# Hybrid decoder step: output product begun on half the tokens, taps' input in 8 transfers, late slots in the scan

## Chip, cores, metric

One Trainium2 chip, one core. The metric is the device time of one execution in microseconds (us); the kernel before took 1579.87 us, median of three runs (1579.34 to 1582.29).

## The reference

One inference step of a two-layer trunk for 512 prompt tokens and 8 x 8 sample tokens, which share the weights; model width 1024. In short:

```python
# layer 0 (even mixer)
a_val, a_gate, q, k, v = split(rmsnorm(x) @ w_in)
u = a_val * sigmoid(a_gate)
c = silu(layernorm(causal_dwconv(concat(conv_hist, u), conv_w, conv_b), ln_g, ln_b))   # width 31, 512 channels
o = sliding-window attention (window 128, 8 query heads on 2 key heads, sinks, partial rotary)
x = x + concat(c, o) @ w_out
x = x + conv_ffn(rmsnorm(x))             # gate, width-3 depthwise conv, silu, times up, down
# layer 1 (odd mixer)
z, xbc, dt = split(rmsnorm(x) @ w_in)
xs, B, C = split(silu(causal_dwconv(concat(hist, xbc))))   # width 4
y, new_state = ssd_scan(xs, softplus(dt + bias), -exp(a_log), B, C, state)   # chunks of 128, 32 heads, 4 groups
y = grouped_rmsnorm((y + d_skip * xs) * silu(z))
x = x + y @ w_out
x = x + conv_ffn(rmsnorm(x))
```

Besides the two outputs the new histories and states are returned: last convolution rows, last 128 keys and values, scan states.

## The kernel before

**Layout.** Features lie on partitions, the 576 tokens (512 + 64) on the free axis, processed as two halves of 288 (`HALF`). Every dense product runs as three matmuls in a split float32 form, `mm3`: weights and activations are each cut into a high part (a copy on ScalarE, L150 for weights, L170 for activations) and a rest (a subtraction on VectorE, L151 and L171); then high x high (L160), high x rest (L161), rest x high (L162). Weights come in 512 KB loads (L141) into three rotating buffers. `units` computes input projections one 128-row output tile at a time; `out_proj` does an output product tile by tile and half by half and adds each result to the residual x on VectorE (`add_x`, L259). The order of instructions on each engine is made when the kernel is built, by a planner that knows the dependencies; SP (SyncE) issues all transfers in one queue, in order.

**Slots.** Most working tiles come from a pool of 48 equal slots in SBUF, 59 after the first mixer. `S` takes the slot that was freed longest ago and `free` puts one at the end of the list. A tile that takes a slot waits until the last reader of the slot's former tile is done, a store included.

**First mixer (`mix0`).** Input projections for gate and value of four channel tiles i = 0 to 3, keys, values, queries; between them attention in blocks of 128 queries: `scores` (with softmax on VectorE, ScalarE and GpSimd), then `values` (transposes L648, copies `ptb` L650, product `po` L653, results `of` L661). The width-31 convolution runs on VectorE for channel tiles 0 and 2 (`conv_taps`, L436, one instruction per tap) and on TensorE for 1 and 3 (`pe_conv`). `pe_conv` writes the padded channel tile to DRAM (`cad`) and loads it back four times, shifted by 0 to 3 tokens, for each of four groups of 32 channels: 32 transfers (L551, L552), each of 32 rows. Eight tap steps follow, each with four 32-column matmuls side by side (L559 for prompt, L566 for sample tokens). After the last block (`sample_scores`, `values(3)`, `sample_values`) `of` is split into pairs `oh`, the LayerNorm over 512 channels runs (mean by matmuls with a matrix of 1/512, L758, squares L762, `rstd` with L182 and L193, scale L765, swish L766, split into `cc`), then the output product for the attention rows (on `oh`), and at last that for the Conformer rows (on `cc`, pairs `ch` and `cl` in the profile).

**Second mixer (`mix1`).** Four groups of eight heads. `ssd(g)` is a generator with 28 steps: it builds chunk states `hst` and stores the final one (`ssm_p`, L1001), then per pair of heads loads decay rows (`acb`, L1018, and `ea2`, L1031, from DRAM), turns them into decays (ScalarE L1022 and L1023, VectorE L1024) and multiplies them into `yp` (L1048). Sample states `h0` are loaded (L1063), updated (L1090) and stored (`ssm_s`, L1091). `run(main, side)` lets the generator go step by step and emits side work between: in group 0 four gate units (z) and two B/C units, in groups 1 and 2 the eight output tiles of the group before and then four gate units, in group 3 gate units and four output tiles, evenly spread over 30 steps. The previous group's eight split tiles are freed with the eighth output tile. `gate` then gates, normalizes and splits.

Of the kernel before, what the change touches and what calls it, by code (L numbers as in the profile page):

```python
# [8 lines left out]
F32 = mybir.dt.float32  # L9
# [41 lines left out]
class Builder:  # L51
# [3 lines left out]
    def __init__(self, nc, tc, d, stack):  # L55
        self.nc, self.tc, self.d = nc, tc, d
        self.const = stack.enter_context(tc.tile_pool(name="const", bufs=1))
        self.xp = stack.enter_context(tc.tile_pool(name="xp", bufs=1))
        self.wp = stack.enter_context(tc.tile_pool(name="wp", bufs=1))
        self.sp = stack.enter_context(tc.tile_pool(name="sp", bufs=1))  # L60
        self.pp = stack.enter_context(tc.tile_pool(name="pp", bufs=1, space=bass.MemoryType.PSUM))
        self.dp = stack.enter_context(tc.tile_pool(name="dp", bufs=1, space=bass.MemoryType.DRAM))
        self.rings = {"mm": [0, 1, 2, 3], "aux": [4, 5, 6, 7]}
        self.idle = list(range(self.NSLOT))
        self.used = {}


    def S(self, name, n=T, dt=F32, rows=P):

        i = self.idle.pop(0)  # L70
# [5 lines left out]
    def free(self, *tiles):  # L76
        for t in tiles:
            if isinstance(t, (list, tuple)):
                self.free(*t)
            else:  # L80
                self.idle.append(self.used.pop(id(t))[0])

# [269 lines left out]
    def mix0(self):  # L352
# [22 lines left out]
        def a_gate(i):  # L375
            def go(half, p):
                if half == 0:
                    sg[i] = self.S("sg")
                    cap[i] = self.segp.tile([P, 542], F32, tag="capp", bufs=1, name="cap") if i in PC else self.S("cap", 542)
# [9 lines left out]
        segs = {}  # L389
        PC, NPTB = (1, 3), 3  # L390

        cad = {i: self.dp.tile([P, 846], F32, name=f"cad{i}") for i in PC}

# [9 lines left out]
        def a_val(i):  # L403
            def go(half, p):
# [3 lines left out]
                else:  # L408
# [5 lines left out]
                    if i in PC:  # L414
                        nc.sync.dma_start(cad[i][:, 0:542], cap[i])
                        nc.sync.dma_start(cad[i][:, 542:846].rearrange("p (b c) -> p b c", c=38), cas_v[i])
                    else:
# [119 lines left out]
        def pe_conv(i):  # L537
# [7 lines left out]
            xs4 = [xsp[c // 2][:, (c % 2) * 304:(c % 2) * 304 + 304] for c in range(4)]  # L545
            src = cad[i]
            for c in range(4):
                for j in range(4):
                    n = 540 if j < 3 else 536
                    r, rc = slice(j * 32, j * 32 + 32), slice(c * 32, c * 32 + 32)  # L550
                    nc.sync.dma_start(xp4[c][r, 0:n], src[rc, j:j + n])  # L551
                    nc.sync.dma_start(xs4[c][r, 0:304 - j], src[rc, 542 + j:846])  # L552
            yield
            pp, ps = self.pm(), self.pm()
            for s in range(8):
                k = slice(0, P if s < 7 else 96)
                for c in (3, 2, 1, 0):
                    w = w4[s // 4][k, (s % 4 * 4 + c) * 32:(s % 4 * 4 + c) * 32 + 32]
                    m = nc.tensor.matmul(pp[c * 32:c * 32 + 32, :], w, xp4[c][k, 4 * s:4 * s + NP], start=s == 0, stop=s == 7)  # L559
                    if s or c < 3:  # L560
                        self.tc.keep_in_program_order(m)
            for s in range(8):
                k = slice(0, P if s < 7 else 96)
                for c in range(4):
                    w = w4[s // 4][k, (s % 4 * 4 + c) * 32:(s % 4 * 4 + c) * 32 + 32]
                    m = nc.tensor.matmul(bt(ps[c * 32:c * 32 + 32, 0:64]), w, xs4[c].rearrange("p (b t) -> p b t", t=38)[k, :, 4 * s:4 * s + 8],  # L566
                                         start=s == 0, stop=s == 7)
# [164 lines left out]
        self.units([then_taps(val_unit(3), 2)], 1)  # L732
        self.norm_end()
        sample_scores()
# [8 lines left out]
        oh = [self.pair("o") for _ in range(4)]  # L743
        for j in range(4):
            self.split(of[j], oh[j])
        self.free(of)
# [3 lines left out]
        some_taps(99)  # L750
        lrs = self.S("lrs")
        csq = [self.S("csq") for _ in range(4)]
        cc = [self.pair("c") for _ in range(4)]
        for half in (0, 1):
            sl = HALF[half]
            pm = self.ps("pm")
            for i in range(4):
                nc.tensor.matmul(pm[:, :HB], self.o512, ca[i][:, sl], start=i == 0, stop=i == 3)  # L758
            for i in range(4):
                nc.vector.tensor_tensor(ca[i][:, sl], ca[i][:, sl], pm[:, :HB], op=SUB)  # L760
# [8 lines left out]
        self.free(oh, list(ca.values()), cas, lrs, csq)  # L769
        self.norm_begin("norm_f0", True)  # L770
# [4 lines left out]
    def mix1(self):  # L775
# [139 lines left out]
        def ssd(g):  # L915
# [85 lines left out]
            nc.sync.dma_start(d["ssm_p"][g], H[3])  # L1001
            self.free(H.pop(), btok)
            yield
# [79 lines left out]
            def finish(bh, behind):  # L1083

                for b4 in range(4):
# [71 lines left out]

        def run(main, side):
# [13 lines left out]
        for g in range(4):  # L1172
# [3 lines left out]
            if g:  # L1176
# [20 lines left out]
            run(ssd(g), side)  # L1197
            ys = gate(g, xs)
# [18 lines left out]
def build(nc, tc, d):  # L1217
    from contextlib import ExitStack
    with ExitStack() as stack:
# [15 lines left out]
def constants():  # L1235
# [12 lines left out]
    put("prot", prot)  # L1248
    put("m32", np.tile(np.eye(32, dtype=f), (4, 1)))
    half = np.arange(P) // 64  # L1250
# [131 lines left out]
```

## Time and profile before

| | |
|---|---|
| median of three runs | 1579.87 us |
| the profiled execution | 1580.21 us, span 1578.4 us, mean granted clock 0.997 |
| TensorE busy | 1547.4 us (98%) |
| VectorE busy | 997.7 us (63%) |
| ScalarE busy | 642.0 us (41%) |
| GpSimd busy | 146.9 us (9%) |
| HBM read, written | 140.54 MB, 15.21 MB |

The span is one profiled execution, from the first to the last instruction. Busy shares are means over stages with different limits; a stage is read by its own stretch of time. PE is TensorE's matmuls, PEld its weight loads, DVE VectorE, ACT ScalarE, POOL GpSimd, SP the queue of transfers. A row of stretches gives start:end, length, busy us (and instructions) of PE, PEld, DVE, ACT, POOL, then the granted TensorE clock as a share of full speed, the DMA share and GB/s. A row of the order of time gives start, duration, engine, line, what is written from what, and in brackets how long the engine had been idle and what ended that. A row of groups gives a count, busy us and mean ns. A float32 matmul shows as two records.

### The profile page before, as it was taken

What the parts mean: (1) busy time and instruction counts of PE and PEld (TensorE: products, weight loads), DVE (VectorE), ACT (ScalarE), POOL (GpSimd) and SP (SyncE); (2) the same over time, 40 slices, a digit from 0 to 9 for tenths busy, and PEclk for the clock granted to TensorE, in tenths of its full rate; (3) what the DMA queues carried; (4) which work ended last, traced back from release to release, by engine and by line L of the source; (5) the groups of instructions that cost most, each with busy time, mean ns of one, the idle gap of its engine ahead of it and who ended that gap; (6) DMA issues with size and microseconds to landing.
All of it is one profiled execution on the core that took longest, in us unless ns stands there. A gap on an engine that the chain in (4) does not pass through costs nothing. (4 is left out here: it accounts for less than half of the span.)

```text
span 1578.4 us, 28672 instructions
## 1 busy us (share of the span) xinstructions
PE 1547.4 (98%) x11709; PEld 1478.0 (94%) x11709; DVE 997.7 (63%) x1750; ACT 642.0 (41%) x1197; POOL 146.9 (9%) x362
## 2 busy tenths in 40 slices
PE   8999999999999999999998999999999999999999
PEld 7966799999999999998997998998999999999998
DVE  7968586553465355677796777776975653653552
ACT  6257373221222122476765555556542321221220
POOL 0026001000000000011202002002010000000000
PEclk9999999999999999999999999999999999999999
DMA  7514223222222222225345235235322222222222
GB/s 224 127 43 111 75 69 103 87 88 81 81 80 82 93 78 76 78 83 162 122 123 163 94 106 178 94 110 171 112 81 81 81 81 81 89 77 91 81 84 76
DMA packets 69841, 157.60 MB, mean 100 GB/s; under 512 B 20158, under 2 KB 24510, under 8 KB 69710
## 3 DMA queue, kind: packets, MB, share of 16 engines
q1 hardware_dynamic: 69710, 155.77, 32.2%
q8 instruction: 92, 1.51, 0.4%
q14 instruction: 39, 0.32, 0.1%
HBM read 140.54 MB, written 15.21 MB: 99 GB/s over the span
## 5 line engine op out<-in xcount | busy, mean ns | idle before, releaser
L160 PE MATMUL mm<-hh,wh 128*128 128x288 f32 (+1 forms) x2288 | 681.6, 298 | 9.0 <-ACT wh L150 7.7
L162 PE MATMUL mm<-hh,wl 128*128 128x288 f32 x2288 | 679.9, 297 | 0.0
L161 PE MATMUL mm<-hl,wh 128*128 128x288 f32 (+1 forms) x2288 | 678.6, 297 | 0.0
L160 PEld LDWEIGHTS mm<-hh,wh 128*128 128x128 f32 (+1 forms) x2288 | 430.2, 188 | 15.1 <-ACT wh L150 8.2
L150 ACT ACTIVATE wh<-wr 128x1024 fp32r<-128x1024 f32 (+1 forms) x215 | 223.4, 1039 | 537.8 <-issue 265.4
L161 PEld LDWEIGHTS mm<-hl,wh 128*128 128x128 f32 (+1 forms) x2288 | 430.9, 188 | 2.0 <-DVE hl L360 0.3
L162 PEld LDWEIGHTS mm<-hh,wl 128*128 128x128 f32 x2288 | 429.8, 188 | 2.9 <-issue 1.5
L151 DVE TENSOR_TENSOR wl<-wr,wh 128x1024 fp32r<-128x1024 f32 (+1 forms) x215 | 259.8, 1209 | 81.5 <-ACT wh L150 81.3
L161 PE MATMUL mm<-yl,wh 128*128 128x288 f32 x960 | 287.0, 299 | 0.2 <-DVE yl L171 0.2
L160 PE MATMUL mm<-yh,wh 128*128 128x288 f32 x960 | 286.3, 299 | 0.7 <-DVE x L259 0.7
L162 PE MATMUL mm<-yh,wl 128*128 128x288 f32 x960 | 284.5, 297 | 0.4 <-DVE wl L151 0.4
L160 PEld LDWEIGHTS mm<-yh,wh 128*128 128x128 f32 x960 | 181.6, 190 | 4.3 <-DVE x L259 1.8
L161 PEld LDWEIGHTS mm<-yl,wh 128*128 128x128 f32 x960 | 182.0, 190 | 2.8 <-issue 1.4
L162 PEld LDWEIGHTS mm<-yh,wl 128*128 128x128 f32 x960 | 181.6, 189 | 1.6 <-issue 0.9
L259 DVE TENSOR_TENSOR x<-x,mm 128x288 f32<-128x288 f32 x192 | 85.3, 451 | 153.1 <-PE mm L162 152.8
L304 DVE TENSOR_TENSOR gbuf<-mm,rs 128x224 f32<-128x224 f32 x44 | 17.2, 391 | 108.9 <-PE mm L162 108.9
L315 ACT ACTIVATE gsilu<-gconv,par 128x512 f32<-128x512 f32 x44 | 31.8, 724 | 115.8 <-DVE gconv L312 115.8
L312 DVE SCALAR_TENSOR_TENSOR gconv<-gbuf,par,gconv 128x592 f32<-128x592 f32 x88 | 73.1, 831 | 1.5
L325 DVE TENSOR_TENSOR gsilu<-mm,gsilu 128x288 f32<-128x288 f32 x88 | 40.0, 455 | 50.7 <-PE mm L162 50.7
L801 DVE SCALAR_TENSOR_TENSOR cconv<-cbuf,par,cconv 128x600 f32<-128x600 f32 x72 | 60.2, 840 | 11.6 <-ACT cconv L799 10.7
L1022 ACT ACTIVATE acb<-acb,ac 128x128 f32<-128x128 f32 x128 | 41.4, 390 | 50.6 <-DMA acb<-acd 34.4
L307 POOL COPY fpo<-gbuf 128x2 f32<-128x2 f32 x44 | 12.4, 281 | 476.0 <-DVE gbuf L304 476.0
(306 smaller groups left out, 1603.1 us busy)
## 6 DMA issues: line engine op xcount, KB each, us to landing
wr<-in_w_gate SPq DMA_DIRECT2D x44, 512.0 KB, 3.3
wr<-in_w_up SPq DMA_DIRECT2D x44, 512.0 KB, 3.3
wr<-in_w_in_o SPq DMA_DIRECT2D x40, 512.0 KB, 3.4
wr<-in_w_down SPq DMA_DIRECT2D x32, 448.0 KB, 3.4
wr<-in_w_down SPq DMA_DIRECT2D x16, 512.0 KB, 3.6
acb<-acd SPq DMA_DIRECT2D x32, 256.0 KB, 4.2
h<-in_h SPq DMA_DIRECT2D x32, 256.0 KB, 3.7
out_ssm_s<-h SPq DMA_DIRECT2D x32, 256.0 KB, 2.4
```

The lines of the kernel that those rows point to most:

```text
L150: nc.scalar.activation(hi[:, :n], raw[:, :n], AF.Copy)
L151: nc.vector.tensor_tensor(lo[:, :n], raw[:, :n], hi[:, :n].bitcast(F32), op=SUB)
L160: nc.tensor.matmul(out, hi[:, ws], xh[:, sl], start=i == 0, stop=False)
L161: nc.tensor.matmul(out, hi[:, ws], xl[:, sl], start=False, stop=False)
L162: nc.tensor.matmul(out, lo[:, ws], xh[:, sl], start=False, stop=i == n - 1)
L259: nc.vector.tensor_tensor(self.x[m][:, sl], self.x[m][:, sl], p[:, :HB], op=ADD)
L304: nc.vector.tensor_tensor(g[:, 290:514], p[:, 0:224], rs[:, HB:NP], op=MUL)
L312: nc.vector.scalar_tensor_tensor(cv[:, :592], g[:, k:592 + k], w(k), cv[:, :592], op0=MUL, op1=ADD)
L315: nc.scalar.activation(sl[:, :NP], cv[:, :NP], AF.Silu, bias=b)
L325: nc.vector.tensor_tensor(sl[:, HALF[half]], p[:, :HB], sl[:, HALF[half]], op=MUL)
L801: nc.vector.scalar_tensor_tensor(cv[:, :600], g[:, k:600 + k], w(k), cv[:, :600], op0=MUL, op1=ADD)
L1022: nc.scalar.activation(acb[:, cs], acb[:, cs], AF.Relu, bias=ac[:, o:o + 1], scale=-1.0)
```

## The change

In the first mixer:

- `oh` is made in two halves. The first half of the output product's tiles 0 to 5 is emitted between the last attention steps (`o_tile`, `o_split`), the second half and tiles 6 and 7 after the LayerNorm.
- The LayerNorm adds the four channel tiles on VectorE first (`lsum`, and the squares into `csq[0]`), so that one matmul each, in place of four, forms mean and square sums.
- `pe_conv` loads its input in 8 transfers: each reads 32 rows of `cad` at four shifts by one access pattern and writes 128 partitions, now ordered channel by shift. `cad` rows have 850 columns, with a zero after the prompt part and three zeros at the end, written by two small stores; the taps' weights and the constant `m32` are reordered to match, and the last tap step uses all 128 rows, with a zero weight for the 32nd tap.

In the slots: each free slot has a turn number, and `S` takes the lowest. `free(..., late=n)` puts a slot n turns further back; used for the final chunk state (8) and the sample states (6), both freed while their store is under way. The 11 extra slots enter with turn 0, ahead of the others.

In the second mixer `run` gets explicit places: over 28 steps, in groups 1 and 2 the output tiles in the first half (at k/16) and the gate units in the second (at 0.5 + k/8); in group 0 at k/6, in group 3 at (k+1)/9.

```diff
+        i = self.idle.pop(self.idle.index(min(self.idle, key=lambda e: e[0])))[1]
+        self.taken += 1
...
-                self.idle.append(self.used.pop(id(t))[0])
+                self.idle.append((self.taken + late, self.used.pop(id(t))[0]))
...
-        cad = {i: self.dp.tile([P, 846], F32, name=f"cad{i}") for i in PC}
+        cad = {i: self.dp.tile([P, 850], F32, name=f"cad{i}") for i in PC}
+        for i in PC:
+            nc.sync.dma_start(cad[i][:, 847:850], zeros)
...
             for c in range(4):
-                for j in range(4):
-                    n = 540 if j < 3 else 536
-                    r, rc = slice(j * 32, j * 32 + 32), slice(c * 32, c * 32 + 32)
-                    nc.sync.dma_start(xp4[c][r, 0:n], src[rc, j:j + n])
-                    nc.sync.dma_start(xs4[c][r, 0:304 - j], src[rc, 542 + j:846])
+                for t, o, n in ((xp4[c], 0, 540), (xs4[c], 543, 304)):
+                    rows = cad[i][c * 32:c * 32 + 32, o:o + n]
+                    nc.sync.dma_start(t[:, 0:n], bass.AP(tensor=rows.tensor, offset=rows.offset,
+                                                         ap=[list(rows.ap[0]), [1, 4], [1, n]]))
...
+        oh = [self.pair("o") for _ in range(4)]
+        wo = {}
+        def o_tile(m, half):
+            if m // 2 not in wo:
+                wo[m // 2] = self.weights(d["w_out_e"][1, m // 2], 1024)
+            p = self.pm()
+            self.mm3(p[:, :HB], wo[m // 2], [(m % 2) * 4 + k for k in range(4)], oh, HALF[half])
+            self.add_x(m, half, p)
...
+        o_split(0)
         sample_scores()
         next(convs[3])
         some_taps(5)
+        o_tile(0, 0)
+        o_tile(1, 0)
         values(3, p3)
         some_taps(5)
+        for m in range(2, 6):
+            o_tile(m, 0)
         sample_values()
         for _ in convs[3]:
             pass
...
-            for i in range(4):
-                nc.tensor.matmul(pm[:, :HB], self.o512, ca[i][:, sl], start=i == 0, stop=i == 3)
+            nc.vector.tensor_tensor(lsum[:, sl], ca[1][:, sl], ca[0][:, sl], op=ADD)
+            for i in (2, 3):
+                nc.vector.tensor_tensor(lsum[:, sl], lsum[:, sl], ca[i][:, sl], op=ADD)
+            nc.tensor.matmul(pm[:, :HB], self.o512, lsum[:, sl], start=True, stop=True)
...
-            self.rstd(lrs, csq, self.o512[:, 0:1], sl)
+                if i:
+                    nc.vector.tensor_tensor(csq[0][:, sl], csq[0][:, sl], csq[i][:, sl], op=ADD)
+            self.rstd(lrs, csq[:1], self.o512[:, 0:1], sl)
...
-        self.out_proj([d["w_out_e"][1, c] for c in range(4)], oh, 4)
+        for m in range(6):
+            o_tile(m, 1)
+        for m in (6, 7):
+            for half in (0, 1):
+                o_tile(m, half)
...
-            self.free(H.pop(), btok)
+            self.free(H.pop(), late=8)
+            self.free(btok)
...
-                    self.free(h0[bh][b4])
+                    self.free(h0[bh][b4], late=6)
...
-            n, k = 30, 0
+            n, k = 28, 0
...
-                while k < len(side) * (i + 1) // n:
+                while k < len(side) and at[k] * n < i + 1:
...
-                side = single(zu) + [last_h] + ot[:4] if g == 3 else ot + single(zu)
+                if g == 3:
+                    side, at = single(zu) + [last_h] + ot[:4], [k / 9 for k in range(1, 10)]
+                else:
+                    side, at = ot + single(zu), [k / 16 for k in range(8)] + [0.5 + k / 8 for k in range(4)]
...
-                side = single(zu + bc_units(1))
+                side, at = single(zu + bc_units(1)), [k / 6 for k in range(6)]
...
-        b.idle += range(b.NSLOT, b.NSLOT + b.EXTRA)
+        b.idle += [(0, i) for i in range(b.NSLOT, b.NSLOT + b.EXTRA)]
```

More of the change, by code (lines that the diff above doesn't have):

```diff
@@ L63, in __init__ @@
         self.rings = {"mm": [0, 1, 2, 3], "aux": [4, 5, 6, 7]}
-        self.idle = list(range(self.NSLOT))
+        self.idle = [(0, i) for i in range(self.NSLOT)]
         self.used = {}
+        self.taken = 0
     def S(self, name, n=T, dt=F32, rows=P):
-        i = self.idle.pop(0)
+        i = self.idle.pop(self.idle.index(min(self.idle, key=lambda e: e[0])))[1]
+        self.taken += 1
         pool = self.sp if i < self.NSLOT else self.ep
@@ L74, in S, with free @@
         return t
-    def free(self, *tiles):
+    def free(self, *tiles, late=0):
         for t in tiles:
             if isinstance(t, (list, tuple)):
-                self.free(*t)
+                self.free(*t, late=late)
             else:
-                self.idle.append(self.used.pop(id(t))[0])
+                self.idle.append((self.taken + late, self.used.pop(id(t))[0]))
     def Z(self, name, n, rows=P, bufs=2):
@@ L733, in mix0, with o_split @@
         self.norm_end()
+        oh = [self.pair("o") for _ in range(4)]
[6 more added lines that the diff above has]
+            self.add_x(m, half, p)
+        def o_split(half):
+            for j in range(4):
+                self.split(of[j][:, HALF[half]], oh[j], HALF[half])
+        o_split(0)
         sample_scores()
@@ L742, in mix0 @@
         self.rings = {"mm": [2, 3, 0, 1], "aux": [4, 5, 6, 7]}
-        oh = [self.pair("o") for _ in range(4)]
-        for j in range(4):
-            self.split(of[j], oh[j])
+        o_split(1)
         self.free(of)
@@ L767, in mix0 @@
                 self.split(ca[i][:, sl], cc[i], sl)
-        self.out_proj([d["w_out_e"][1, c] for c in range(4)], oh, 4)
-        self.free(oh, list(ca.values()), cas, lrs, csq)
+        for m in range(6):
[3 more added lines that the diff above has]
+                o_tile(m, half)
+        self.free(oh, list(ca.values()), cas, lrs, lsum, csq)
         self.norm_begin("norm_f0", True)
```

31 lines of the change are left out of this document (16 added, 15 removed).

## The prediction

> **What bounds the kernel now.** I read the page's first part, then the stretches of 20 us for the granted clock, then what TensorE waited for, and last the order of time around each wait.
>
> ```profile
> span 1578.4 us, 28672 instructions
> PE 1547.4 (98%) x11709; PEld 1478.0 (94%) x11709; DVE 997.7 (63%) x1750; ACT 642.0 (41%) x1197; POOL 146.9 (9%) x362
> 400.00:420.00 20.00, 20.00 (x153) 20.00 (x152) 7.09 (x10) 3.83 (x5) 0.95 (x8) 1.00 0.25 80
> PE yp L1048 <- DVE acb L1024: 7.9, 4, 2.7
> ```
>
> TensorE sets the time. In the feed-forward stretch it issues 152 to 153 matmuls of 288 columns in 20 us, 0.131 us each, with no gap. So time can only come from matmul work taken away or from waits removed. Its longest wait lies in the second mixer's scan (below); the gap that comes next lies at the first mixer's attention end (columns: start, us, and in brackets the idle time before):
>
> ```profile
> 147.74 0.29 PE L162 MATMUL mm<-hh,wl 128*128 128x288 f32 x1
> 150.21 0.42 PE L684 MATMUL sc<-kct,qss 64*32 64x128 f32 x8 [0.45 <-DVE mx L605]
> 156.37 1.88 PE L653 MATMUL po<-ptb,vt 128*64 128x512 f32 x4 [3.06 <-ACT ptb L650]
> 165.34 0.53 PE L160 MATMUL mm<-oh,wh 128*128 128x288 f32 x2 [0.55 <-ACT oh L170]
> 166.13 0.40 PE L161 MATMUL mm<-ol,wh 128*128 128x288 f32 x1 [0.26 <-DVE ol L171]
> 153.00:156.00 3.00, 0.32 (x2) 0.00 (x0) 3.00 (x10) 2.99 (x12) 0.00 (x0) 1.00 0.75 86
> 156.00:160.00 4.00, 3.63 (x12) 1.69 (x12) 3.89 (x8) 1.40 (x3) 3.83 (x4) 0.57 0.34 79
> ```
>
> From the end of the input projections (147.9) to the output product's steady stream (166.1), TensorE is idle 0.45 + 3.06 + 0.55 + 0.26 = 4.3 us, and after the long gap its clock is 0.57 for 4 us: 0.43 x 4 = 1.7 us lost. Together 6.0 us. From 153 to 156 VectorE and ScalarE are full (3.00 and 2.99 of 3 us), so only TensorE work that needs little of them can fill it.
>
> **The change, part by part.** *Half-token products.*
>
> ```profile
> 143.11 0.79 ACT L661 ACTIVATE of<-po 128x128 f32<-128x128 f32 x4 [1.18 <-PE po L653]
> 153.05 1.22 DVE L151 TENSOR_TENSOR wl<-wr,wh 128x1024 fp32r<-128x1024 f32 x1
> ```
>
> Six tiles on the first 288 tokens, 12 matmuls x 0.131 = 1.57 us each, 9.4 us in all, move from behind the attention into this stretch. Their tokens come from blocks 0 to 2; block 2's values are out at 143.9, and the third of their weight tiles is converted by 154.3. They cost nothing new on TensorE; 9.4 us more than covers the 4.3, and without the long gap the 1.7 should go. Gain 6.0 us; at the least 2 if the two "mm" banks must wait for additions queued behind VectorE's taps. The halved split is eight pieces instead of four, under 1 us more on VectorE, and the earlier additions delay the taps by some 2 us; both lie before the convolution's end. The fourth weight tile has to wait for the first one's second half, which now comes behind the convolution; five half tiles (7.9 us) then cover its conversion.
>
> *Fewer float32 matmuls in the LayerNorm.*
>
> ```profile
> 184.54 1.24 PE L758 MATMUL pm<-ca,o 128*128 128x288 f32 x4
> 185.40 0.51 PE L160 MATMUL mm<-oh,wh 128*128 128x288 f32 x1
> 188.17 1.61 PE L182 MATMUL pt<-o,csq 128*96 128x1 f32 x18
> 189.64 0.38 PE L162 MATMUL mm<-oh,wl 128*128 128x288 f32 x1
> L758 PE MATMUL pm<-ca,o 128*128 128x288 f32 x16 | 5.1, 419 | 0.0
> L182 PE MATMUL pt<-o,csq 128*96 128x1 f32 x48 | 4.8, 215 | 0.0
> 185.33 3.01 DVE L760 TENSOR_TENSOR ca<-ca,pm 128x288 f32<-128x288 f32 x8 [0.39 <-PE pm L758]
> ```
>
> Summing on VectorE first leaves 4 of the 16 mean records and 12 of the 48 square-sum records (each float32 matmul is two records). Start to start, four mean records take 0.86 us (0.215 each) and eighteen of the others 1.47 (0.082 each). Saved: 12 x 0.215 + 36 x 0.082 = 2.6 + 2.9 = 5.5 us of TensorE. It adds 12 additions of 288 columns on VectorE, 3.01 / 8 = 0.38 each, 4.6 us; at least the last sum of each kind, twice 0.38, is in series.
>
> *Taps' input in 8 transfers.*
>
> ```profile
> 156.52 0.32 SPq L551 DMA_DIRECT2D xp<-cad  x1
> 171.73 0.42 SPq L552 DMA_DIRECT2D xs<-cad  x1
> 176.59 7.08 PE L559 MATMUL mm<-xp,w 128*32 128x512 f32 x64
> xp<-cad SPq DMA_DIRECT2D x24, 67.5 KB, 2.0
> acb<-acd SPq DMA_DIRECT2D x32, 256.0 KB, 4.2
> 156.50:173.70 17.20, 16.39 (x119) 11.88 (x120) 11.26 (x18) 5.70 (x18) 3.61 (x4) 0.90 0.48 107
> 848.00:852.00 4.00, 4.00 (x34) 4.00 (x33) 3.42 (x6) 2.06 (x4) 0.00 (x0) 1.00 0.98 335
> ```
>
> First and last of 32 issues lie 15.2 us apart, 0.49 each: the queue's issue time, not the bytes, holds the convolution to 176.6. Eight issues end about 160.4. The bytes, 128 rows x (540 + 304) x 4 x 4 = 1.73 MB, take 7.8 us at 107 / 0.48 = 223 GB/s and 5.2 at 335, so with 2.0 to land the input is there between 163.7 and 166.3. TensorE gets to the convolution after what it did between 147.9 and 165.3 (17.4, less 4.1 idle, 1.7 of clock and 1.7 of mean records now gone: 9.9) and the six half tiles: 147.9 + 9.9 + 9.4 = 167.2. So I take no wait; an output weight load falling between the transfers could make it 1. At the first convolution SP sheds 24 issues too, but TensorE does not wait there, so nothing. 128 rows instead of 96 in the last tap step change no matmul's columns: nothing. The two stores of three zero columns are two issues of 0.3 to 0.5 us on SP near the start: below 1 us, I take 0.
>
> *The tail.* Moved products no longer cover the LayerNorm.
>
> ```profile
> 183.74 0.75 DVE L570 TENSOR_SCALAR ca<-mm,par 128x512 f32<-128x512 f32 x1 [6.58 <-PE mm L559]
> 206.54 0.82 DVE L171 TENSOR_TENSOR cl<-ca,ch 128x288 fp32r<-128x288 f32 x2
> 206.94 0.29 PE L160 MATMUL mm<-ch,wh 128*128 128x288 f32 x1
> ```
>
> Before, the chain from the convolution's eviction to the last split took 23.6 us (183.74 to 207.36), and TensorE went into the Conformer product at 206.94 without a gap. Now the eviction starts at 167.2 + 7.2 = 174.4, and the same chain ends at 198.0. TensorE would be there at 206.94 - 6.0 - 5.5 = 195.4, and needs the second half of the tokens one tile later, 197.0. So 1.0 us comes back. It is 0 if the chain closes up, and 1.0 + 4.6 = 5.6 if every added addition lies in series. I take 1.0. First mixer: -6.0 - 5.5 + 1.0 = -10.5, between -11.5 and -2.
>
> *Late slots.*
>
> ```profile
> 841.10 0.44 PE L1048 MATMUL yp<-acb,xdt 128*64 128x128 f32 x4 [2.68 <-DVE acb L1024]
> 857.78 0.33 PE L1048 MATMUL yp<-acb,xdt 128*64 128x128 f32 x2 [1.71 <-DVE acb L1024]
> 959.95 0.33 PE L1048 MATMUL yp<-acb,xdt 128*64 128x128 f32 x2 [1.60 <-DVE acb L1024]
> 1090.51 0.33 PE L1048 MATMUL yp<-acb,xdt 128*64 128x128 f32 x2 [1.92 <-DVE acb L1024]
> 828.43 0.34 SPq L1001 DMA_DIRECT2D out_ssm_p<-hst  x1
> 834.40 0.32 SPq L1018 DMA_DIRECT2D acb<-acd  x1
> SPq L1018 <- DMA out_ssm_p<-hst: 5.5, 1, 5.5
> SPq L1018 <- DMA out_ssm_p<-hst: 3.4, 1, 3.4
> 840.00:848.00 8.00, 6.90 (x45) 6.50 (x46) 5.90 (x10) 1.60 (x5) 0.00 (x0) 0.79 0.64 164
> 1090.50:1098.00 7.50, 7.49 (x51) 6.90 (x51) 5.23 (x9) 7.47 (x17) 0.00 (x0) 0.77 0.37 141
> ```
>
> In groups 1 and 2 the load of a decay row stands in SP's queue for 5.5 and 3.4 us, because its slot still holds the final state that is being stored; h loads and the rest of the queue stand behind it. The products at 841.10 and 959.95 are the ones that come up short (2.68 and 1.60 us). A later turn for that slot takes both waits away. After 841.10 the clock loses 0.21 x 8 = 1.7 more. Gain 2.68 + 1.60 + 1.7 = 6.0. The other two (1.71; 1.92 with again 0.23 x 7.5 = 1.7 of clock) have other causes, and I leave them.
>
> *Output tiles first, the extra slots, 28 steps.* In groups 1 and 2 the eight output tiles (24 x 0.131 = 3.1 us each) now fall into the first 13 of 28 steps, and the four gate units (6.3 us) are spread to step 25. The previous group's eight slots come free before the scan's outputs start; the scan's second half has 28 us of cover instead of 32 and one unit fewer behind it. The order on every queue is made anew, and a trace of the old order cannot price that: between a gain of the remaining 1.71 + 1.92 + 1.7 = 5.3 and a loss like the one stall seen with its clock, 2.68 + 1.7 = 4.4. I take +2.0, one stall the size of those seen. The extra eleven slots being taken first only moves the feed-forward history's load, which has tens of us before its use. Second mixer: -6.0 + 2.0 = -4.0, between -11.3 and +4.4.
>
> Each long gap lost 1.7 us of clock, and gaps of 1.71 and 1.60 lost none; 1.92 was enough. [...]
>
> **The sum.** The profiled execution took 1580.21 us, span 1578.4, 0.34 above the median of 1579.87. 1580.2 - 10.5 - 4.0 = 1565.7, less 0.3 for the median: 1565.4.
>
> **Rivals.** *First mixer only.* The new order in the second mixer gives back what the late slots win. For it: four waits with different causes. 1579.9 - 10.5 = 1569.4.
>
> *The gain ends in the tail.* The LayerNorm chain, not TensorE, sets when the Conformer product starts, and the second mixer gives nothing. The chain ends at 198.0 only if the convolution starts at 167.2; if its input is late by 8 us, where it nearly is now, it ends at 206.0, with two added sums in series at 206.8, and the product starts at 205.2, 1.7 earlier than before: 1578. Against it: issues are 0.49 us and 24 of them go.
>
> *Slower: the eight transfers run one behind the other.* A 256 KB load took 4.2 us to land. Eight in series are 33.6 us: the convolution starts at 156.5 + 33.6 = 190.1, its eviction at 197.3, the chain ends at 220.9, and the Conformer product starts one tile before that, at 219.3, 12.4 us later than now. 1579.9 + 12.4 - 4.0 = 1588. It decides above some 3.5 us each (28 in all). Against: transfers 0.49 apart that land in 2.0 overlap already.
>
> *Slower: the new order starves the scan.* A stall like that at 841.10, 4.4 us with its clock, four times in the four groups, with the late slots' gain lost too, is +17.6 against -10.5: 1587; it decides above three. Against: TensorE has 28 us of cover there.
>
> *Everything goes right*, all four scan waits and no tail: -11.5 - 11.3, 1557.
>
> **Chances.** Forecast 0.62; first mixer only 0.15; all goes right 0.05; tail 0.08; serial transfers 0.05; starved scan 0.05. A change under 0.2% (3.2 us) is about what cannot be told from none here. Faster 0.82, same 0.08, slower 0.10. The range runs from 1558 to 1577, the first mixer alone at its poorer end included.
>
> **What would show it.** Right: no gap over 1 us before the po product; the first convolution of xp's second turn near 167; 4 pm and 12 csq records; the ch products from about 196; no wait of an acb load on out_ssm_p. Wrong: xp landing after 168; a gap before the first ch product over 3 us; new yp waits in groups 0 to 3, above all with the clock below 1.00 behind them.

## The result and the profile after

The changed kernel takes 1570.68 us (median of four runs, 1570.16 to 1572.56) against 1579.77 (1579.34 to 1582.29) for the kernel before: a ratio of 0.9945, interval 0.9932 to 0.9959. That is 9.1 us faster by the medians; 14.5 were forecast, and the time lies inside the forecast range of 1558 to 1577. The profiled execution took 1572.56 us, span 1570.8, 1.9 above its median.

The gain came from the first mixer alone, as the experiments below show. The page's head of the changed kernel:

```profile
span 1570.8 us, 28493 instructions
PE 1543.0 (98%) x11661; PEld 1476.0 (94%) x11661; DVE 1001.3 (64%) x1766; ACT 640.6 (41%) x1201; POOL 162.0 (10%) x365
```

TensorE has 48 matmul records fewer, 4.4 us less busy time and, with the span 7.6 us shorter, 3.2 us less idle time. Its order of time around the attention's end and at the Conformer product (start, us, line, and in brackets the idle time before, where there is one; line numbers have moved, so that L163 is the old L160 and L1081 the old L1048):

```profile
158.14 1.08 PE L659 MATMUL po<-ptb,vt 128*64 128x512 f32 x4
166.81 1.05 PE L566 MATMUL mm<-xp,w 128*32 128x512 f32 x2
169.32 1.06 PE L566 MATMUL mm<-xp,w 128*32 128x512 f32 x8
196.88 0.30 PE L163 MATMUL mm<-ch,wh 128*128 128x288 f32 x1
```

Its stretches there (start:end, length, busy us of PE, PEld, DVE, ACT, POOL, then clock, DMA share, GB/s):

```profile
140.00:180.00 40.00, 39.16 (x383) 27.33 (x382) 34.05 (x72) 16.52 (x47) 16.71 (x14) 1.00 0.35 93
162.00:166.00 4.00, 4.00 (x33) 4.00 (x32) 3.85 (x8) 0.47 (x3) 0.00 (x0) 1.00 0.83 280
166.00:170.00 4.00, 3.97 (x54) 2.05 (x56) 2.39 (x4) 1.75 (x9) 0.00 (x0) 1.00 0.02 7
```

The 3.06 us before the last block's first `po` product are gone (no bracket at 158.14), TensorE is busy 39.16 of 40 us at a clock of 1.00, and the Conformer product starts at 196.88 instead of 206.94: 10.1 us earlier. The first and the last of the eight issues of the taps' input, from SP's order of time:

```profile
156.45 0.56 SPq L559 DMA_DIRECT2D xp<-cad  x1
161.12 0.60 SPq L559 DMA_DIRECT2D xs<-cad  x1
```

They are 0.67 us apart and end at 161.7. From 162 to 166 the DMA engines move 280 GB/s, and from 166 on 0.02 of them is busy. The input is there when TensorE arrives at 166.8.

The second mixer added nothing to that. The store of `acr` (the row that heads the scan) is issued at 688.8 against 699.4, 10.6 us earlier, and the last store of the second feed-forward at 1504.05 against 1511.48: only 7.4 earlier. So the stretch between got 3 us longer in these two executions, where 4 us less were forecast. That is near the spread of single executions: the same stretch is 3.1 us shorter than before in the run with the first mixer only (below), where the second mixer has no edit. TensorE's waits for a decay row (us in total, times, longest), the two rows in order of time, and the stretches behind them:

```profile
PE yp L1081 <- DVE acb L1057: 6.9, 2, 4.2
```

```profile
757.38 1.97 PE L1081 MATMUL yp<-acb,xdt 128*64 128x128 f32 x16 [4.18 <-DVE acb L1057]
1081.42 1.97 PE L1081 MATMUL yp<-acb,xdt 128*64 128x128 f32 x16 [2.71 <-DVE acb L1057]
```

```profile
756.00:764.00 8.00, 6.62 (x38) 6.30 (x39) 5.62 (x7) 5.35 (x10) 1.39 (x3) 0.57 0.31 92
1080.00:1088.00 8.00, 6.58 (x34) 5.99 (x35) 5.83 (x9) 7.98 (x20) 3.72 (x3) 0.57 0.37 143
```

Before there were four `yp` waits, 7.9 us, three of them in groups 1 and 2. Those three are gone. In their place group 0 waits 4.18 us where it did not wait, and group 3 waits 2.71 instead of 1.92. Behind each of the two the clock stands at 0.57 for 8 us: 0.43 x 8 = 3.4 us lost each, twice what a long gap cost in the kernel before.

What stands in group 0's way is seen in the order of time of the two engines that make a decay row, ScalarE and VectorE (the data of the first row had landed at 749.3; the last line is a load of a decay row):

```profile
749.33 1.28 ACT L1055 ACTIVATE acb<-acb,ac 128x128 f32<-128x128 f32 x4 [3.44 <-DMA acb<-acd]
750.52 0.33 ACT L827 ACTIVATE cbuf<-mm 128x224 f32<-128x224 f32 x1
751.38 0.79 ACT L831 ACTIVATE cconv<-cbuf,par 128x600 f32<-128x600 f32 x1
752.07 1.56 ACT L1055 ACTIVATE acb<-acb,ac 128x128 f32<-128x128 f32 x5
753.53 0.62 ACT L1056 ACTIVATE acb<-acb 128x512 f32<-128x512 f32 x1
752.71 1.62 DVE L833 SCALAR_TENSOR_TENSOR cconv<-cbuf,par,cconv 128x600 f32<-128x600 f32 x1
754.72 1.15 DVE L833 SCALAR_TENSOR_TENSOR cconv<-cbuf,par,cconv 128x600 f32<-128x600 f32 x1
755.79 1.52 DVE L1057 TENSOR_TENSOR acb<-acb,cbm 128x512 f32<-128x512 f32 x1
753.04 0.33 SPq L1051 DMA_DIRECT2D acb<-acd  x1
```

The groups of the two VectorE lines in the whole kernel (duration in ns, least, median and most):

```profile
L833 DVE SCALAR_TENSOR_TENSOR cconv<-cbuf,par,cconv x72: 809/843/1618, 668.2 to 1037.8; 128x600 f32<-128x600 f32 x72
L1057 DVE TENSOR_TENSOR acb<-acb,cbm x32: 675/691/1530, 715.2 to 1092.5; 128x512 f32<-128x512 f32 x32
```

L827 to L833 are the width-4 convolution of the next group's first B/C unit. With the new places that unit falls inside the loop over decay rows, and its work stands among theirs in both queues, in order. The two convolution steps of 1.62 and 1.15 us take over half of VectorE's time while `yp` waits (753.2 to 757.4); by the medians they would be 0.84 each, and the decay product (L1057, the decays times `cbm`) 0.69 instead of 1.52. A load of a decay row stands in SP's queue at the same time, 3.1 us, for the slot of a sample state that is still being stored. It is not what `yp` waits for: it is issued at 753.04, when ScalarE has been at work since 752.07 on the row that VectorE takes up at 755.79.

### The profile page after: what moved, and what is told of

It reads as the page before. It is cut to its first block, busy times and chain, and to the rows that moved or that the text cites. A ratio compares the mean times of both kernels' runs of the same rounds, so it can differ in the third digit from the quotient of the medians.

```text
span 1570.8 us, 28493 instructions
## 1 busy us (share of the span) xinstructions
PE 1543.0 (98%) x11661; PEld 1476.0 (94%) x11661; DVE 1001.3 (64%) x1766; ACT 640.6 (41%) x1201; POOL 162.0 (10%) x365
## 4 chain that ended last, share of the span: by engine, by line
PE 85%; DVE 4%; ACT 3%; DMA 1%; issue 1%; POOL 0%; SPq 0%; ACTq 0%; POOLq 0%; DVEq 0%
PE mm L165 25%; PE mm L163 25%; PE mm L164 25%; PE mm L566 1%; PE yp L1081 1%; PE pst L1023 1%; ACT acb L1055 1%; DMA acb<-acd 1%; DVE cconv L833 1%; DVE ca L446 1%; PE pt L1010 1%; PE py L1068 1%; PE pst L1122 0%; PE pt L185 0%; PE pr L196 0%
## 5 line engine op out<-in xcount | busy, mean ns | idle before, releaser
L163 PE MATMUL mm<-hh,wh 128*128 128x288 f32 (+1 forms) x2288 | 683.1, 299 | 7.0 <-ACT wh L153 6.6
L164 PE MATMUL mm<-hl,wh 128*128 128x288 f32 x2288 | 679.1, 297 | 0.1
L163 PEld LDWEIGHTS mm<-hh,wh 128*128 128x128 f32 (+1 forms) x2288 | 430.9, 188 | 11.8 <-ACT wh L153 6.8
L164 PEld LDWEIGHTS mm<-hl,wh 128*128 128x128 f32 x2288 | 432.0, 189 | 3.0 <-issue 0.7
L163 PE MATMUL mm<-yh,wh 128*128 128x288 f32 x960 | 287.6, 300 | 2.2 <-ACT cbuf L828 1.4
L163 PEld LDWEIGHTS mm<-yh,wh 128*128 128x128 f32 x960 | 181.2, 189 | 4.6 <-ACT cbuf L828 1.6
L833 DVE SCALAR_TENSOR_TENSOR cconv<-cbuf,par,cconv 128x600 f32<-128x600 f32 x72 | 61.3, 853 | 15.3 <-ACT cconv L831 14.5
L310 POOL COPY fpo<-gbuf 128x2 f32<-128x2 f32 x44 | 12.4, 283 | 471.4 <-DVE gbuf L307 471.4
```

Source lines behind the costliest of these rows:

```text
L163: nc.tensor.matmul(out, hi[:, ws], xh[:, sl], start=i == 0, stop=False)
L164: nc.tensor.matmul(out, hi[:, ws], xl[:, sl], start=False, stop=False)
L833: nc.vector.scalar_tensor_tensor(cv[:, :600], g[:, k:600 + k], w(k), cv[:, :600], op0=MUL, op1=ADD)
```

## The experiments

Every time stands beside the kernel before on the same chip (medians there 1579.8 us for the change, and 1579.5, 1580.6 and 1580.2 in the three series of the other runs). Kernels of different series are compared by their ratios; by these intervals a difference of two ratios is uncertain by some 0.002, 3 to 4 us.

| run | us | ratio (interval) |
|---|---|---|
| the change | 1570.68 | 0.9945 (0.9932 to 0.9959) |
| first mixer only | 1566.88 | 0.9915 (0.9900 to 0.9931) |
| second mixer only | 1577.57 | 0.9988 (0.9978 to 0.9997) |
| group 0's last unit behind | 1576.08 | 0.9978 (0.9969 to 0.9987) |
| no late turns | 1571.55 | 0.9946 (0.9932 to 0.9960) |
| first mixer, 32 transfers | 1575.21 | 0.9961 (0.9947 to 0.9975) |
| first mixer, LayerNorm as before | 1575.84 | 0.9970 (0.9956 to 0.9984) |
| first mixer, products behind | 1578.89 | 0.9992 (0.9982 to 1.0003) |
| group 0's places as before | 1566.57 | 0.9910 (0.9893 to 0.9927) |
| all places as before | 1566.46 | 0.9914 (0.9896 to 0.9932) |
| B/C units late | 1570.05 | 0.9935 (0.9915 to 0.9954) |
| B/C units late, group 3 as before | 1568.97 | 0.9927 (0.9910 to 0.9944) |

**Which half gives.** The first mixer's edits with slots and places of the second as before, and the reverse.

```diff
 # first mixer only: beside the run() of before (30 steps, even places)
-  b.idle += [(0, i) for i in range(b.NSLOT, b.NSLOT + b.EXTRA)]
+  b.idle += [(b.taken, i) for i in range(b.NSLOT, b.NSLOT + b.EXTRA)]
...
-  self.free(H.pop(), late=8); self.free(btok)
+  self.free(H.pop(), btok)
...
-  self.free(h0[bh][b4], late=6)
+  self.free(h0[bh][b4])
 # second mixer only: the kernel before with the three lines marked - and the new places of the change
```

> All edits of the first mixer; slots and places of the side work in the second mixer as before. Theory A (the first mixer gave all of the gain, the second mixer's edits together nothing or a small loss): the Conformer product starts near 196.9 as in the changed kernel, 10 us earlier than before, and the time is 1569.5 us or a little less than the changed kernel's 1570.7, with the yp waits of before (four, 7.9 us) still there. Rival B (the second mixer's edits gain as forecast, 4 us, and the first mixer loses some of its 10 us further on): the time is above 1573.

> Turn numbers with late slots, the extra slots first, and the new places of the side work; the first mixer as before. Theory A: 1579 to 1582 us, no gain: no decay row waits for the stored final state any more, but group 0 has a wait of about 4 us at yp with the clock halved behind it, and group 3 one of 2 to 3 us. Rival B: 1575 to 1576 us.

The first mixer alone gives 12.7 us (1579.5 to 1566.9), 2.6 more than the expected 1569.5 stands for; the second alone gives 2.0, which lies between its two expectations; both together give 9.1. Of the 12.7, 11.3 lie ahead of the `acr` store in the profiled execution (688.1 against 699.4), and its unchanged scan had `yp` waits of 6.3 us instead of 7.9. So the second mixer's edits cost 4.7 us by the ratios (0.9945 less 0.9915) once the first's are in. In the run of the second mixer alone the stall in group 0 is there as well (this row is from its order of time on TensorE):

```profile
766.26 1.98 PE L1052 MATMUL yp<-acb,xdt 128*64 128x128 f32 x16 [4.31 <-DVE acb L1028]
```

**Slots, late turns, or places?**

```diff
 # group 0's last unit behind
-  side, at = single(zu + bc_units(1)), [k / 6 for k in range(6)]
+  side, at = single(zu + bc_units(1)), [k / 6 for k in range(5)] + [1.0]
 # no late turns: the two free() lines above alone
```

> The changed kernel, but in group 0 the sixth side unit (the second B/C unit of the next group) stands behind the scan, as before, not at 5/6 of it. Theory A1 (that unit takes two slots just ahead of the last decay row, which then gets the slot of the last sample state, still being stored): the wait of 4.2 us at yp in group 0 and the two stretches of half clock behind it, 3.4 us, go: 1563 to 1566 us. Rival A2 (the wait comes from the order on the transfer queue or the cover, whichever slot it takes): a wait of similar size stays, 1569 to 1572.

> The changed kernel without late turns: the final state's and the sample states' slots come back in the plain order; places and first mixer as changed. If the late turns are what took the waits out of groups 1 and 2: decay rows wait for the stored final state again, 3 to 6 us on the queue in each group, yp waits of 2 to 3 us return, 1574 to 1577 us. Rival (the places did it, since the output tiles first free eight slots early): groups 1 and 2 stay without yp waits, within 1.5 us of 1570.7.

With the sixth unit behind the scan the wait at the same product is still 4.21 us, and the time is worse: in that trace new waits of 1.59 and 1.20 us come up at 778.7 and 780.7, where the unit now stands, with the clock at 0.57 on average from 780 to 792. So the sixth unit was the wrong one to move: it is the fifth, the first B/C unit, that stands at the decay rows of 749 to 757. Without late turns the time is the same, and groups 1 and 2 still have no long `yp` wait, although the acb loads wait on the state's store again, if for less than the 8.9 us of the kernel before (the waits of SP's queue, then those of TensorE, in the run without late turns):

```profile
SPq L1050 <- DMA out_ssm_p<-hst: 4.6, 3, 2.6
```

```profile
PE yp L1080 <- DVE acb L1056: 7.2, 3, 4.1
```

So in the changed kernel the new order is enough to take the waits out of groups 1 and 2, and beside it the late turns are worth nothing that shows.

**Group 0's places.**

```diff
 # group 0's places as before: steps 5, 10, 15, 20, 25 and behind
-  [k / 6 for k in range(6)]
+  [4.5 / 28, 9.5 / 28, 14.5 / 28, 19.5 / 28, 24.5 / 28, 1.0]
 # B/C units late: only the two B/C units at their former places
+  [k / 6 for k in range(4)] + [24.5 / 28, 1.0]
 # group 3 as before, beside that
-  [k / 9 for k in range(1, 10)]
+  [((30 * k + 8) // 9 - 0.5) / 28 for k in range(1, 9)] + [1.0]
 # all places as before
-  n, k = 28, 0
+  n, k = 30, 0
...
-  while k < len(side) and at[k] * n < i + 1:
+  while k < len(side) * (i + 1) // n:
```

> The whole change (1570.7 us), with only group 0's six side units put back to steps 5, 10, 15, 20, 25 and behind the scan. Theory (the first unit of the next group's B and C, with its convolution on ScalarE and VectorE, stands among the decay rows of group 0): the 4.2 us wait of yp in group 0 and the 3.4 us of clock behind it go, 1563 to 1565 us, and acr's store to the last state's store takes some 7 us less. Rival (the stall belongs to what the new slots and the changed order of later groups make of the queues, and not to the place of that unit): the wait stays in group 0 or one like it comes up in groups 1 to 3, 1569 to 1572 us.

> The whole change, with group 0's four gate units at the new places and its two B and C units at the former ones, step 25 and behind the scan. Theory (the B/C unit's convolution work stands among the decay rows in the queues of ScalarE and VectorE): the 4.2 us wait of yp in group 0 is gone, and also the 2.7 us wait of a pst product that the former gate places showed; ratio 0.988 to 0.991. Rival (the gate units come too early and leave the later steps without cover for TensorE): a wait of 2 us or more stays in group 0 behind step 15, ratio 0.993 to 0.995.

> As the run with the B and C units late, and group 3's nine side units also at their former steps 4, 7, 10, 14, 17, 20, 24, 27 and behind. Theory: the 2.7 us wait of yp in group 3 shrinks to the 1.9 us of the kernel before, 0.8 us less and at times 1.7 to 3.4 us of clock: ratio 0.987 to 0.990. Rival: group 3's wait does not hang on the places, no difference to the run with the B and C units late within its interval.

> The whole change with all side units at their former places: the first mixer's edits, the late turns and the extra slots' turn 0. Theory (only the new places cost): it stands no worse than the first mixer alone, and the late turns take the acb waits on out_ssm_p out of groups 1 and 2, worth at most 1 us as the run without late turns showed: ratio to the kernel before 0.990 to 0.992, 1564 to 1567 us. By the prediction's own term the late turns are worth 6.0 us: ratio 0.988, 1561 us. Rival (the late turns or the extra slots cost something): 1569 us or more.

Group 0's places alone bring back 5.5 us by the ratios (0.0035 of 1580), and the wait of `yp` in group 0 is gone. From `acr`'s store to the last state's store that trace takes 6.8 us less, as expected, but not all of it comes from group 0: 3.4 us are clock that the changed kernel lost behind group 3's gap of 2.71 us and this one did not (last section). Moving only the two B/C units takes the wait in group 0 away too, and moving the second of them alone did not. So the place of the first one, alone or with the second, is the wait's cause. That it acts through the queues of ScalarE and VectorE is read from the rows shown above; no run moved its work in one queue alone. Their profiles show what comes in its place (waits of TensorE: first with all six units back, where the one `yp` wait is group 3's, then with the B/C units alone late; `pst` is the product that updates a sample state, L1010 belongs to the chunk states):

```profile
PE pst L1122 <- DVE ea L1070: 2.7, 1, 2.7
PE yp L1081 <- DVE acb L1057: 2.7, 1, 2.7
```

```profile
PE pst L1122 <- DVE h L1123: 5.4, 4, 2.3
PE pt L1010 <- DVE xdt L1012: 1.9, 1, 1.9
```

The expected ratio of 0.988 to 0.991 with the B/C units late was missed (0.9935, which lies in the rival's range): two waits came up in group 0 instead, 1.92 us at the chunk states and 1.90 at a `pst` product, and one of 2.33 in group 1. That the gate units come too early there is thus not excluded. The gain over the change, 0.0010, is within the intervals. Group 3's former steps brought its wait from 2.7 to 2.0 in the profile, but the time did not change within the interval. And late turns with all places as before stand at 0.9914, the first mixer alone at 0.9915. There the state's store no longer holds up the loads of `acb` but those of `h0` (L1096), again by SP's waits:

```profile
SPq L1096 <- DMA out_ssm_p<-hst: 8.0, 3, 3.6
```

The later turn handed the slot to another load in the same queue. In that run the `yp` waits of group 1 are down to 0.5 us, from 2.6 in the first mixer alone, but others have grown (`pst` in group 0 from 1.79 to 2.72, `yp` in group 3 from 1.92 to 2.28, and one of 1.0 at L982), and the time is the same. No version beat the first mixer alone by more than the intervals; two stand level with it at 0.991.

**The first mixer's terms, one by one.** Each run takes one edit out of the first mixer alone.

```diff
 # 32 transfers (cad layout and weights' order as before, too)
-  for t, o, n in ((xp4[c], 0, 540), (xs4[c], 543, 304)):
+  for j in range(4):
+      nc.sync.dma_start(xp4[c][r, 0:n], src[rc, j:j + n])
+      nc.sync.dma_start(xs4[c][r, 0:304 - j], src[rc, 542 + j:846])
 # LayerNorm as before (no sums on VectorE)
-  nc.tensor.matmul(pm[:, :HB], self.o512, lsum[:, sl], start=True, stop=True)
+  for i in range(4):
+      nc.tensor.matmul(pm[:, :HB], self.o512, ca[i][:, sl], start=i == 0, stop=i == 3)
...
-  self.rstd(lrs, csq[:1], self.o512[:, 0:1], sl)
+  self.rstd(lrs, csq, self.o512[:, 0:1], sl)
 # products behind
-  o_split(0)
...
-  o_tile(0, 0); o_tile(1, 0)
...
-  for m in range(2, 6): o_tile(m, 0)
...
-  for m in range(6): o_tile(m, 1)
-  for m in (6, 7):
+  for m in range(8):
       for half in (0, 1): o_tile(m, half)
```

> First mixer alone (1566.9 us), with the taps' input loaded in 32 transfers again. Theory: 32 issues of 0.49 us from about 156.5 on end at 172, so the last data land near 174 and the second turn's convolution cannot start before 174 to 176.6, where it starts at 167 to 169 with 8 transfers. TensorE has nothing else in its order there, so it waits 6 to 9 us and loses 1.7 or 3.4 us of clock behind that: 1574 to 1579 us, the first Conformer product at 204 to 207. Rival: the input is there in time anyhow or the wait is covered by the products that follow: 1567 us, first Conformer product near 197.

> First mixer alone (1566.9 us), with the LayerNorm's sums made by four matmuls each again: 16 mean records and 48 square-sum records in place of 4 and 12. Theory (TensorE's time is what counts): the 5.5 us of float32 matmuls return in full, 1572.4 us, first Conformer product 5.5 us later, near 202. Rival (the chain on VectorE sets the product's start): the twelve added sums of 0.38 us leave that chain and the matmuls fit into its waits, 1565 to 1567.5 us.

> First mixer alone (1566.9 us), with the whole output product of the attention rows behind the LayerNorm again. Theory: the gaps before and after the last attention block return (4.3 us idle and 1.7 of clock), and TensorE reaches the second turn's convolution 3 us earlier than with the products ahead, near 163.8, where the input is there at 165.5 to 166: some 2 us of a new wait. Together 6 to 8 us: 1573 to 1575 us, with a gap of about 3 us before the first po product of the last block. Rival: the planner fills the gap with other work and the moved products only change places: 1567 us.

With 32 transfers the size was met (1575.2 us; 7.3 more by the ratio) and the place was not. The issues, from SP's order of time, then TensorE's rows and stretches:

```profile
155.06 0.32 SPq L555 DMA_DIRECT2D xp<-cad  x1
169.94 0.42 SPq L556 DMA_DIRECT2D xs<-cad  x1
```

```profile
168.14 0.53 PE L163 MATMUL mm<-oh,wh 128*128 128x288 f32 x2 [1.00 <-ACT oh L173]
178.98 7.08 PE L563 MATMUL mm<-xp,w 128*32 128x512 f32 x64
200.65 0.61 PE L163 MATMUL mm<-ch,wh 128*128 128x288 f32 x1 [3.25 <-ACT ch L173]
```

```profile
168.00:176.00 8.00, 7.86 (x46) 7.67 (x47) 5.53 (x11) 2.14 (x5) 0.00 (x0) 0.79 0.42 116
200.00:208.00 8.00, 7.35 (x32) 7.07 (x33) 6.33 (x16) 6.65 (x18) 0.73 (x3) 0.57 0.29 90
```

The last issue comes 14.9 us after the first. The wait of 6 to 9 us that was expected ahead of the convolution does not open: the order made for this kernel puts the second half tiles in front of it, after a gap of 1.00 us, and starts the convolution at 178.98. Those tiles are then missing at the tail, where TensorE waits 3.25 us for `ch`. The clock loses 0.21 x 8 = 1.7 and 0.43 x 8 = 3.4 us behind the two.

With the LayerNorm of before, `pm` has 16 records and `csq` 48 again, and the Conformer product starts at 202.04, 5.2 us later than with the first mixer alone (196.84). That is the 5.5 us of matmuls; the rival, that the shorter chain on VectorE makes up for them, fell. The time is 8.7 us worse by the ratio. The other 3 us are about the uncertainty of the two ratios; in the two profiled executions the stretch behind the `acr` store is longer too, by 4.3 us, with `yp` waits of 8.1 us instead of 6.3, and no run says why.

With the products behind, the gap before `po` is back, and TensorE now reaches the convolution ahead of its input (order of time, then stretches):

```profile
157.58 1.97 PE L659 MATMUL po<-ptb,vt 128*64 128x512 f32 x4 [3.56 <-ACT ptb L656]
165.99 1.30 PE L566 MATMUL mm<-xp,w 128*32 128x512 f32 x8 [2.04 <-DMA xp<-cad]
208.16 0.30 PE L163 MATMUL mm<-ch,wh 128*128 128x288 f32 x1
```

```profile
156.00:164.00 8.00, 6.36 (x20) 2.46 (x20) 7.82 (x13) 3.85 (x13) 4.27 (x4) 0.57 0.55 167
164.00:176.00 12.00, 10.01 (x88) 4.13 (x92) 5.39 (x9) 3.56 (x12) 0.00 (x0) 0.72 0.25 85
```

3.56 + 2.04 us idle, 0.43 x 8 + 0.28 x 12 = 6.8 us of clock: 12.4 us. The product starts 11.3 us later than with the first mixer alone. The run took 12.2 us more by the ratio, some 4 above what was expected: the places of the two gaps were as expected and their lengths nearly, and the clock took 6.8 us where 1.7 had been counted.

The three edits taken out one at a time cost 7.3 + 8.7 + 12.2 = 28.2 us, and all three together gave 13.4 by the same measure (0.0085 of 1580). They lean on each other: with 8 transfers TensorE would wait for the input unless the products fill the time, and with 32 the products are used up before the convolution and leave the tail bare.

## Why the prediction was right, and where it was wrong

The forecast's first half, -10.5 in the first mixer, held; its second half, -4.0 in the second mixer, did not: it came out at +3.6 (12.7 less 9.1). That the time is only 5.3 us off is in part luck, since the first mixer gave 2.2 more than its term.

*Half-token products, transfers, tail: right, in time and in mechanism.* Forecast were the convolution at 167.2, its eviction at 174.4, the end of the last split at 198.0 and the Conformer product at 196.4. The first mixer's convolution starts at 166.81 and 169.32, interleaved with the sample values; the product comes at 196.88 without a gap. The tail, by the order of time on VectorE:

```profile
176.45 0.75 DVE L576 TENSOR_SCALAR ca<-mm,par 128x512 f32<-128x512 f32 x1 [2.92 <-PE mm L566]
197.59 0.82 DVE L174 TENSOR_TENSOR cl<-ca,ch 128x288 fp32r<-128x288 f32 x2
```

The eviction is 2.0 us later than forecast, and the chain takes 22.0 us (176.45 to 198.41) instead of 23.6: even with the added sums it is no longer than before. The two errors nearly cancel, which is luck. The input was costed at 163.7 to 166.3 and the queue falls quiet near 166; the eight transfers, issued 0.67 us apart, landed 3.9 (`xp`) and 3.7 us (`xs`, both medians) after their issue, so they did not run one behind the other.

*Fewer matmuls: right.* 4 and 12 records, and 5.2 us at the Conformer product when they are put back, for 5.5 forecast.

*Each step's price by itself: not what the terms say.* The forecast added the steps (-6.0, -5.5, transfers only as a wait avoided). Their sum held (-10.5 against 10.1 in the trace, 12.7 in the time of the first mixer alone), but taking any one away costs more than its term; for the products and the transfers the traces show the waits that then open elsewhere. Without the products TensorE stands 2.04 us before the taps' input, and the clock loses 6.8 us where the term of -6.0 holds 1.7.

*Late slots, -6.0: wrong.* The step that failed is that the waits of the acb loads in SP's queue were read as the cause of the short products at 841.10 and 959.95. In the first mixer alone those loads still wait for the state's store (7.3 us, longest 3.8), and the product that had been 2.68 us short is 0.87 short. Taking the late turns out of the change leaves 4.6 us of those waits in the queue and no loss in time; keeping them with the old places shortens group 1's `yp` waits and gains nothing. The term measures 0, within 3 to 4 us.

*New order, +2.0: mis-sized.* The prediction took one stall of 2.0 and named, as what would prove it wrong, "new yp waits in groups 0 to 3, above all with the clock below 1.00 behind them". That is what came: 4.18 and 0.79 (2.71 less 1.92) us of idle time, and 3.4 of clock twice where 1.7 was lost once in group 3. Against that stand the waits of groups 1 and 2 that the order took away, 2.68 + 1.71 + 1.60 with 1.7 of clock = 7.7. 4.18 + 0.79 + 3.4 + 1.7 = 10.1, so +2.4 for this account of the scan; the trace has +3. The +2.0 was thus near the net of the order, by luck: it was taken as one stall, where the order took three waits away and brought a new one and a longer one. It was also meant beside a gain of 6.0 from late slots which the order, not they, had brought. The rival "first mixer only" (1569.4, given 0.15) is the case that happened, with the first mixer some 2 us better than its term and the scan worse than nothing. The starved scan needed four stalls; two came.

*The clock.* By the rows of before, 1.7 us per long gap; here gaps of 4.18 and 2.71 lost 3.4 each, and with 32 transfers one of 1.00 us lost 1.7. A gap of one length has several prices, as the last section shows; what sets the price was not shown.

## What to carry to other kernels

When products are moved to fill a gap, ask at once what they covered where they were: here the moved products, the faster loads and the shorter LayerNorm gave some 13 us together, and any two of them without the third only 1 to 6; one alone was not run. A wait in a transfer queue is worth time only if the row it delays is the one that the matmul waits for (here 4.6 us of such waits came back without the late turns, and the ratio was 0.9946 against 0.9945); follow it to that row before it is priced. And in-order queues make the place of a side unit a cost of its own (here, as read from group 0's rows, 4.18 us and 3.4 of clock): a unit whose evictions and convolution run on ScalarE and VectorE doesn't belong among the rows that these engines must deliver next.

## What the runs showed of the hardware that was not expected

The same gap costs clock or does not. Group 3's wait of 2.71 us stands in the changed kernel and in the one with group 0's places as before. In the first the clock behind it is 0.57 for 8 us (1080 to 1088, shown above). In the second it is 1.00 (shown below, order of time and stretch):

```profile
1076.80 1.09 PE L1081 MATMUL yp<-acb,xdt 128*64 128x128 f32 x16 [2.71 <-DVE acb L1057]
```

```profile
1076.00:1084.00 8.00, 6.88 (x58) 6.17 (x60) 7.89 (x13) 7.97 (x18) 3.10 (x3) 1.00 0.37 143
```

The same 16 products take 1.97 us or 1.09. A gap of 2 to 3 us lost 0 here (2.71, with group 0's places as before), 1.7 (2.68, in the kernel before) or 3.4 us (2.71, in the changed kernel). The clock changes from run to run too: with the B/C units late one program took from 1564.78 us at a mean clock of 1.000 to 1573.20 at 0.996. Of these 8.4 us about 0.004 x 1570 = 6.3 are clock. So a gap of 2 us taken away may be worth 2 or nearly three times that (2 + 3.4, an estimate from these rows). What decides between the prices, no run here shows.

VectorE's instructions in the stalled stretch took about twice their usual time: L1057 at 755.79 took 1.52 us and L833 at 752.71 took 1.62, where the medians of these lines are 0.69 and 0.84. GpSimd ran `h<-h,cds` (the decay of the sample states) from 751.2 to 756.8 meanwhile. In the traces of the kernel before and of the changed one the two go together: of their 64 decay products 48 have no `h<-h,cds` beside them, and none takes over 0.70 us; 16 have, and they take 0.69 to 1.57. The convolution step (L833 in the changed kernel) takes 0.87 us at most without it; the two beside it took 1.62 and 1.15. The rows of the stalled stretch, then of the run with group 0's places as before:

```profile
751.20 5.58 POOL L1109 TENSOR_TENSOR h<-h,cds 128x512 f32<-128x512 f32 x4
```

```profile
732.63 4.04 POOL L1109 TENSOR_TENSOR h<-h,cds 128x512 f32<-128x512 f32 x4 [31.38 <-PE pyo L1103]
735.62 1.60 DVE L1057 TENSOR_TENSOR acb<-acb,cbm 128x512 f32<-128x512 f32 x1 [2.25 <-ACT acb L1056]
749.03 5.28 POOL L1109 TENSOR_TENSOR h<-h,cds 128x512 f32<-128x512 f32 x4 [0.29 <-PE pyo L1103]
751.17 0.77 DVE L1057 TENSOR_TENSOR acb<-acb,cbm 128x512 f32<-128x512 f32 x1 [0.21 <-ACT acb L1056]
```

By the medians the four VectorE instructions of these two lines between 751.5 and 757.3 are some 2.5 us longer than usual, so up to that much of the 4.18 us may be GpSimd's (an estimate). No run took GpSimd's work away, and the decay products of 751.17 and 752.71 beside it cost only 0.77 and 0.69: how much of the 4.18 us it is stays open.
